# Expert weights in runs of 16 KB, and activations stored in a permuted order

## The chip, the cores and the metric

One core of one Trainium2 chip runs the whole program; the metric is device microseconds of one execution. Before the change three runs took 1560.23, 1564.00 and 1565.98 us, the median being 1564.0 us.

## The reference, cut to what matters

A sequence of 256 tokens (T) of width 1024 (D) passes two blocks, all in float32.

```
# first block
h   = layer_norm(2**0.25 * x + token_mixer(x), ln1)         # attention and a gated MLP
logits = h @ w_router + b_router                            # 32 experts, the best 4 for each token
for each expert e, on the tokens that chose it:
    gt  = min(xb @ w_gate[e] + b_gate[e], 7)                # w_gate, w_up, w_down: 32 x 1024 x 1024
    up  = clip(xb @ w_up[e] + b_up[e], -7, 7)
    hid = gt * sigmoid(1.702 * gt) * (up + 1)
    y   = hid @ w_down[e] + b_down[e]
x   = layer_norm(2**0.25 * h + sum of y * gate, ln2)
# second block: a recurrent mixer and an attention side by side, then a convolved feed-forward of width 2816
```

## The kernel before, in words

**Stages.** `front` computes the first block up to h and the router, `moe` the experts, `tail_norm` the second layer norm, `mixer2` and `ffn2` the second block. The order of the work on each engine is the order in the code. SP issues nearly all loads, in order; a load into a slot waits on SP until the slot's last reader is done.

**Expert weights.** A matrix of 4 MB (1024 rows of 4 KB) comes in four quarters of 1 MB. Quarter i holds rows 256 i to 256 i + 255, and partition p gets rows 256 i + 2p and 256 i + 2p + 1: one run of 8 KB. So the contraction index of chunk k on partition p is row 256 (k // 2) + 2p + k % 2, and the left operands have to be taken in the same order: `pairs(k)` (line 628) is that slice, with a step of two, used by the gather of h (line 710), by the transposes of the hidden values (line 768) and in the overflow loop. There are 384 quarters; `expert_pieces` gives their order: gate and up of expert e, then down of expert e - 1.

**Slots.** 18 slots of 1 MB each, in two pools, hold quarters in turn. In `front` the same slots serve the first block's weights: `pump` (L1260) loads a raw piece and splits it into two float32r parts (`wp`, L1272 on ACT and L1273 on VectorE or POOL); five slots hold small constants and intermediate results (`carve`). As the slots come free, `through` and `freed` load the first 18 quarters of expert weights. In `moe`, `ahead(n)` calls `fetch`, which issues (L188) the refills of all slots whose readers already stand in the code, so that SP runs 18 quarters ahead.

**An expert.** The experts are taken in turn, two to a batch of 128 gathered rows, 64 for each. `gate_up(e)` runs "gate" (tile g) and "up" (tile u), 8 chunks x 2 halves of 512 columns each, and `swiglu` (L757 to L761); `finish(e - 1)` runs "down" (tile y) of the expert before; `hidden_t` transposes the hidden values. After each second expert `gather` (L707 to L713) picks the next batch's rows with one-hots and `scatter` (L728) adds the results into `self.acc`, which is the tile of x. At expert 0 `start_sum` (L916) writes the gated b_down plus 2**0.25 * h there.

**The end of `front`.** For each of the two halves of 128 tokens the layer norm's scale comes from VectorE's steps L97 to L109; `router` takes the logits (L558), their top 8 (L559), scales h on ACT (L560) and adds ln1_b on POOL (L561). The routing's VectorE chain (L665 to L688) and the one-hots (L700) follow, then the first gather.

**The end of `moe`.** After the last "down", loads of ln2_g, ln2_b and norm1_g go into two slots, and `stream` sets up the second block's loads with six of the slots, two for raw pieces and four for parts.

Of the kernel before, what the change touches and what calls it, by code (L numbers as in the profile page):

```python
# [17 lines left out]
OP = mybir.AluOpType  # L18
# [12 lines left out]

SLOTS_A = "r8 c1 c0 c2 c3 c4".split()
SLOTS_B = "r0 r1 r2 r3 r4 r5 r6 r7 h0 h1 h2 h3".split()

REST = 15
RING_A = len(SLOTS_A)
FFN_RAW, FFN_HALF = 4, 4
# [18 lines left out]
def bcast_rows(ap, n, parts=128):  # L56
    return bass.AP(tensor=ap.tensor, offset=ap.offset, ap=[[0, parts], [1, n]])


class Net:  # L60
# [66 lines left out]
    def run(self):  # L127
# [31 lines left out]
        with ExitStack() as fctx:  # L159
            self.front(fctx)  # L160
        self.dump("h", self.h)
# [19 lines left out]

    def piece(self, src, name="w"):

        pool, i = self.rings[self.turn % len(self.rings)]
        self.turn += 1
        t = pool.tile([128, 2048], F32, tag=i, name=self.nm(name))
        for view, ap in src(t):
            self.nc.sync.dma_start(view, ap)  # L188
        return t

    def front(self, fctx):
# [18 lines left out]

        slot = {i: (p, f"s{i}") for p, names in ((self.pa, SLOTS_A), (self.pb, SLOTS_B)) for i in names}
        cs = [slot[f"c{i}"][0].tile([128, 2048], F32, tag=f"sc{i}", name=f"front_c{i}") for i in range(5)]

# [39 lines left out]
        nf = len(spec)  # L253
        work = self.expert_pieces()
        spec += [(2, src) for _, src in work[:len(slot)]]
        L = {}
# [348 lines left out]
        assert len(self.raw) == len(spec) and not self.raw_slots  # L605
        self.rings = [self.held[nf + i] for i in range(len(slot))]
        self.turn = len(slot)
        self.work = work
        self.got = {key: t for (key, _), t in zip(work, self.raw[nf:])}

# [15 lines left out]

    @staticmethod
    def pairs(k):


        i, x = divmod(k, 2)
        return slice(256 * i + x, 256 * i + 256, 2)

    def expert_pieces(self):

        r = []
        for e in range(NE + 1):
            for x, names in ((e, ("w_gate", "w_up")), (e - 1, ("w_down",)), (e, ("w_down",))):
                if x in range(NE) and (len(names) == 2 or (x == e) == (x == REST)):
                    for nme in names:  # L640
                        v = self.a[nme][0, x].rearrange("(i p x) c -> i p x c", p=128, x=2)
                        r += [((x, nme, i), v[i]) for i in range(4)]
        return r

    def fetch(self, n):

        for key, src in self.work[len(self.got):n]:
            t = self.piece(lambda t: [(t.rearrange("p (k c) -> p k c", k=2), src)])
            self.got[key] = t.rearrange("p (k c) -> p k c", k=2)

    def moe(self, mctx):
# [127 lines left out]
        def weights_of(e, nme):  # L779
            return lambda k: self.got[e, nme, k // 2][:, k % 2, :]  # L780

# [67 lines left out]
        def overflow():  # L849
            n = nc.values_load(lists["num"][0:1, 0:1], min_val=0, max_val=NL - 1)  # L850
            with tc.If(n > 0):
                with tc.For_i(0, n, 1) as i:
# [15 lines left out]
                    for k in range(KC):  # L868
                        for t in range(NT):
                            self.mm(p[:, k, :], self.h[:, t, self.pairs(k)], oh[:, t], start=t == 0, stop=t == NT - 1)  # L870
                    nc.vector.tensor_copy(xo, p)

                    def weights(nme):
                        def f(k):
                            w = m2.tile([128, D], F32, tag="wx", bufs=1, name=self.nm("wx"))
                            rows = a[nme][0, bass.ds(e, 1)].rearrange("o (i p x) c -> i x (o p) c", p=128, x=2)
                            nc.gpsimd.dma_start(w, rows[k // 2, k % 2])
                            return w
# [26 lines left out]
        def start_sum():  # L905
# [18 lines left out]
        def ahead(n):  # L924

            self.fetch(done[0] + len(self.rings))
            done[0] += n

        def finish(e):
            b, el = divmod(e, EB)  # L930
            ahead(4)
            if el == 0:
# [43 lines left out]

        def small(*names):
            while self.rings[self.turn % len(self.rings)][0] is self.pa:
                self.turn += 1
            t = self.piece(lambda t: [(t[:, i * D:(i + 1) * D], bcast_rows(a[nme], D)) for i, nme in enumerate(names)])  # L980
            return t[:, 0:D], t[:, D:2 * D]

        self.ln2g, self.ln2b = small("ln2_g", "ln2_b")
        self.n1g, self.junk = small("norm1_g_2")
        flush(sums)
# [216 lines left out]
    def stream(self):  # L1202
# [23 lines left out]
        for f in range(NF + 2):  # L1226
            for q in range(3):
# [3 lines left out]
                if u % 2 == 0:  # L1231
# [5 lines left out]
                               else (lambda t, x=x: t[:, x:x + 1, :])))  # L1237
        self.pieces(spec, halves, [(self.pa, f"s{i}") for i in SLOTS_A[:2]])
        self.half_slots = [(self.pa, f"s{i}") for i in SLOTS_A[2:]]
        self.low = [self.nc.gpsimd]  # L1240
# [8 lines left out]
    def pump(self):  # L1249

        nc = self.nc
        while True:
            while self.raw_slots and len(self.raw) < len(self.spec):
                r = len(self.raw)
                k, src = self.spec[r]
                pool, tag = self.held[r] = self.raw_slots.pop(0)
                n = src.shape[2]
                t = pool.tile([128, 2048], F32, tag=tag, name=self.nm("w"))[:, :k * n]
                t = t.rearrange("p (k c) -> p k c", k=k)
# [8 lines left out]
            k, n = src.shape[1:]  # L1268
            pool, tag = slot = self.half_slots.pop(0)
            t = pool.tile([128, 2, 1024], F32R, tag=tag, name=self.nm("wp"))[:, :, :k * n]  # L1270
            t = t.rearrange("p q (k c) -> p q k c", k=k)
# [650 lines left out]
    def ffn2(self):  # L1922
# [3 lines left out]
        with ExitStack() as c:  # L1926
# [7 lines left out]

            self.raw_slots += [(ph, f"r{i}") for i in range(FFN_RAW)]
            self.pump()
# [6 lines left out]
            self.low = [V]  # L1943
            self.half_slots += [(ph, f"h{i}") for i in range(FFN_HALF)]
            self.pump()
# [60 lines left out]
```

## Time and profile before

| what | value |
|---|---|
| profiled execution | 1563.47 us |
| its span | 1561.9 us |
| mean granted TensorE clock | 0.973 |
| busy: PE, VectorE, ACT, POOL | 1430.0, 598.6, 364.3, 178.4 us |
| HBM read | 488.34 MB |
| loads of w_gate, w_up, w_down | 128 each, 1024 KB, 19.8 us from issue to landing |

PE is TensorE's matmul, PEld its weight load, DVE VectorE, ACT ScalarE, POOL GpSimd, SP the engine that issues loads (SPq: its queue). L77 is the helper through which all matmuls pass, so they are told apart by tiles: g, u and y are the products of the experts. The DMA share is the mean busy share of 16 engines, and it can pass 1. In the timeline a row has its start, its length, engine, line, operation, and the tiles written and read; in brackets stands the idle time before it and what ended that. Groups have busy us, mean ns of one, and the idle time before.

### The profile page before, as it was taken

How to read it: one execution, taken by the hardware profiler on the slowest of the kernel's cores; microseconds unless marked ns; L12 is line 12 of the kernel's file. 1: busy time of each engine (PE TensorE's matmuls, PEld its weight loads, DVE VectorE, ACT ScalarE, POOL GpSimd, SP SyncE). 2: the span in 40 equal slices, each digit the busy share in tenths (PEclk: the TensorE clock that was granted, in tenths of full speed). 3: DMA queues.
4: the chain of work that ended last, by engine and by line, in shares of the span. 5: the costliest groups of instructions: out<-in, count | busy, mean ns of one | idle time of the engine just before them, and what ended most of it. 6: DMA issues, size and time to landing. Idle time of an engine off the chain costs nothing. (4 is left out here: it accounts for less than half of the span.)

```text
span 1561.9 us, 19367 instructions
## 1 busy us (share of the span) xinstructions
PE 1430.0 (92%) x7904; PEld 823.4 (53%) x7904; DVE 598.6 (38%) x1087; ACT 364.3 (23%) x607; POOL 178.4 (11%) x155
## 2 busy tenths in 40 slices
PE   8779999999998889899988989997998999999998
PEld 7664333333333233233333333326877787799998
DVE  5882121122121121112124111116587547876664
ACT  4551010110101000100110100103643323365552
POOL 4630000000000020000000000004353223200000
PEclk9988999999999999999999999998998999999999
DMA  9886999999999999999999999993423125765540
GB/s 300 289 324 270 423 420 421 422 421 421 422 421 421 421 419 416 422 421 421 422 422 420 421 422 422 421 393 104 149 88 118 32 80 173 239 218 180 194 139 28
DMA packets 119280, 491.15 MB, mean 314 GB/s; under 512 B 16391, under 2 KB 46791, under 8 KB 70036
## 3 DMA queue, kind: packets, MB, share of 16 engines
q1 hardware_dynamic: 118304, 489.02, 78.9%
q8 instruction: 63, 1.03, 0.3%
q10 hardware_dynamic: 372, 0.66, 0.1%
q0 software_dynamic: 512, 0.20, 0.1%
q14 instruction: 29, 0.24, 0.0%
HBM read 488.34 MB, written 1.51 MB: 314 GB/s over the span
## 5 line engine op out<-in xcount | busy, mean ns | idle before, releaser
L77 PE MATMUL u<-w,xg 128*64 128x512 f32 x1024 | 231.5, 596 | 17.3 <-DMA w<-in_w_up_dram 17.3
L77 PE MATMUL g<-w,xg 128*64 128x512 f32 x1024 | 238.3, 613 | 9.4 <-DMA w<-in_w_gate_dram 9.4
L77 PE MATMUL y<-w,hidT 128*64 128x512 f32 x1024 | 228.1, 595 | 6.1 <-DMA w<-in_w_down_dram 5.1
L1273 DVE TENSOR_TENSOR wp<-w,wp 128x1024 fp32r<-128x1024 f32 x115 | 151.4, 1342 | 102.0 <-ACT wp L1272 101.8
L1272 ACT CAST wp<-w 128x1024 fp32r<-128x1024 f32 (+1 forms) x148 | 151.6, 1038 | 163.0 <-PE pj L77 59.0
L77 PEld LDWEIGHTS u<-w,xg 128*64 128x64 f32 x1024 | 68.9, 137 | 170.0 <-issue 119.3
L77 PEld LDWEIGHTS g<-w,xg 128*64 128x64 f32 x1024 | 72.3, 141 | 154.8 <-issue 122.3
L77 PEld LDWEIGHTS y<-w,hidT 128*64 128x64 f32 x1024 | 70.3, 137 | 157.7 <-issue 136.9
L1273 POOL TENSOR_TENSOR wp<-w,wp 128x1024 fp32r<-128x1024 f32 (+1 forms) x33 | 79.3, 2410 | 593.0 <-ACT wp L1272 591.0
L777 ACT COPY y<-y 64x512 f32<-64x512 f32 x64 | 37.1, 580 | 375.9 <-PE y L77 375.4
L757 DVE TENSOR_SCALAR g<-g 128x512 f32<-128x512 f32 x32 | 22.1, 691 | 230.3 <-PE g L77 230.3
L770 DVE COPY hidT<-tr 128x256 f32<-128x256 f32 x32 | 13.6, 425 | 236.5 <-ACT hidT L769 236.5
L760 DVE TENSOR_SCALAR g<-u 128x512 f32<-128x512 f32 x32 | 22.1, 692 | 180.5 <-PE u L77 180.5
L77 PE MATMUL pj<-wp,h2p 128*128 128x512 f32 x336 | 84.4, 408 | 1.1 <-DVE wp L1273 0.9
L758 ACT ACTIVATE sg<-g 128x512 f32<-128x512 f32 x32 | 20.2, 630 | 255.1 <-DVE g L757 255.1
L77 PEld LDWEIGHTS pj<-wp,h2p 128*128 128x128 f32 x336 | 64.1, 194 | 17.8 <-DVE wp L1273 1.3
L77 PE MATMUL a<-h3p,wp 128*128 128x256 f32 x528 | 66.9, 283 | 0.5 <-DVE h3p L1308 0.5
L77 PEld LDWEIGHTS a<-h3p,wp 128*128 128x128 f32 x528 | 66.1, 191 | 2.2 <-DVE h3p L1308 0.7
L77 PE MATMUL b<-h3p,wp 128*128 128x256 f32 x528 | 66.9, 283 | 0.0
L77 PEld LDWEIGHTS b<-h3p,wp 128*128 128x128 f32 x528 | 64.9, 192 | 0.0
L77 PE MATMUL sc<-y,ogT 128*128 128x512 f32 x124 | 62.5, 619 | 2.5 <-ACT y L777 1.4
L77 PE MATMUL d<-wp,hid 128*128 128x512 f32 x264 | 63.6, 391 | 0.0
(527 smaller groups left out, 1582.8 us busy)
## 6 DMA issues: line engine op xcount, KB each, us to landing
w<-in_w_gate_dram SPq DMA_DIRECT2D x128, 1024.0 KB, 19.8
w<-in_w_up_dram SPq DMA_DIRECT2D x128, 1024.0 KB, 19.8
w<-in_w_down_dram SPq DMA_DIRECT2D x128, 1024.0 KB, 19.8
w<-in_w_in_dram SPq DMA_DIRECT2D x27, 1024.0 KB, 5.1
w<-in_w_ffn_up_dram SPq DMA_DIRECT2D x22, 1024.0 KB, 5.3
w<-in_w_ffn_down_dram SPq DMA_DIRECT2D x11, 1024.0 KB, 7.7
w<-in_w_out_dram SPq DMA_DIRECT2D x8, 1024.0 KB, 8.7
w<-in_w_branch_b_dram SPq DMA_DIRECT2D x2, 1024.0 KB, 5.0
```

Of the source, the lines that this page charges most:

```text
L77: return self.nc.tensor.matmul(out, lhsT, rhs, start=start, stop=stop)
L757: nc.vector.tensor_scalar(g1, pg, 7.0, None, op0=OP.min)
L758: nc.scalar.activation(sg, g1, AF.Sigmoid, scale=1.702)
L760: nc.vector.tensor_scalar(g1, pu, -7.0, 7.0, op0=OP.max, op1=OP.min)
L770: nc.vector.tensor_copy(hidT[:, 2:4].rearrange("p j f s -> p j (f s)"), p[:, 2:4])
L777: nc.scalar.copy(yv[64 * i:64 * i + 64, hf * 512:(hf + 1) * 512], py[64 * hf:64 * hf + 64, :])
L1272: nc.scalar.copy(t[:, 0], src)
L1273: self.low[j % len(self.low)].tensor_tensor(t[:, 1], src, t[:, 0].bitcast(F32), op=OP.subtract)
```

## The change

A matrix's halves (2 MB) replace quarters as the unit of most loads: partition p gets rows 512 i + 4p to 512 i + 4p + 3, one run of 16 KB. The 18 slots become nine tiles of 16 KB a partition (`PAIRS`); a half of such a tile is a `Slot`. In `front` and in the second block the halves are used singly. In `moe` the first refill of each tile goes into the same tile by quarters, later ones are single loads into a new tile, and the last four quarters again go singly.

The new order of rows (4p + x) would be a slice with a step of four. Instead the columns of h are stored in the order in which the chunks want them: ACT's scale and POOL's addition in `router` write permuted into the tile of x, which becomes `self.h`, and the tile that was h becomes `self.acc`; VectorE's last step in `swiglu` writes permuted into a new tile `hid`; `start_sum` reads h back through the permutation. The gather and the transposes then take plain slices of 128.

```diff
+PAIRS = "r2r3 r4r5 r6r7 r8c1 c0c2 c3c4 r0r1 h2h3 h0h1".split()
+PAIRS_A = PAIRS[3:6]
+EARLY = 2 * len(PAIRS)
-        self.acc = self.x
+        self.acc, self.h = self.h, self.x
+    def double(self, name, dtype=F32):
+        return (self.pa if name in PAIRS_A else self.pb).tile([128, 4096], dtype, tag=name, name=self.nm("w"))
+    def halved(t):
+        return [Slot(t[:, 2048 * x:2048 * x + 2048]) for x in range(2)]
...
         def freed():
             self.freed()
-            if len(self.half) == len(halves):
-                self.raw_slots += self.half_slots
-                self.half_slots = []
-                self.pump()
+            for name in PAIRS[-2:]:
+                pair = [slot[name[:2]], slot[name[2:]]]
+                if len(self.half) == len(halves) and all(i in self.half_slots for i in pair):
...
+                    through(name[:2], name[2:])
...
-            S.activation(r[:, t, :], r[:, t, :], AF.Copy, scale=rs)
-            G.tensor_tensor(r[:, t, :], r[:, t, :], ln1b, op=OP.add)
+            S.activation(self.by_chunks(self.x[:, t, :]), self.by_rows(r[:, t, :]), AF.Copy, scale=rs)
+            G.tensor_tensor(self.by_chunks(self.x[:, t, :]), self.by_chunks(self.x[:, t, :]), self.by_rows(ln1b), op=OP.add)
...
+    def by_chunks(t):
+        return t.rearrange("q (i x p) -> q i p x", x=4, p=128)
+    def by_rows(t):
+        return t.rearrange("q (i p x) -> q i p x", x=4, p=128)
...
     def fetch(self, n):
-        for key, src in self.work[len(self.got):n]:
-            t = self.piece(lambda t: [(t.rearrange("p (k c) -> p k c", k=2), src)])
-            self.got[key] = t.rearrange("p (k c) -> p k c", k=2)
+        while self.turn < n and 2 * self.turn < len(self.work):
+            u = 2 * self.turn
+            name = PAIRS[self.turn % len(PAIRS)]
+            early = u < 2 * EARLY
+            t = (self.early[name] if early else self.double(name)).rearrange("p (k c) -> p k c", k=4)
+            self.turn += 1
+            (key, src), (key1, src1) = self.work[u:u + 2]
+            if not early and u < len(self.work) - 4:
+                e, nme, q = key
+                v = self.a[nme][0, e].rearrange("(i p x) c -> i p x c", p=128, x=4)
+                self.nc.sync.dma_start(t, v[q // 2])
+            else:
+                self.nc.sync.dma_start(t[:, 0:2], src)
+                self.nc.sync.dma_start(t[:, 2:4], src1)
...
-                    self.mm(p[:, c, :], self.h[:, t, self.pairs(c0 + c)],
+                    self.mm(p[:, c, :], self.h[:, t, (c0 + c) * 128:(c0 + c + 1) * 128],
...
-            nc.vector.scalar_tensor_tensor(sg, g1, 1.0, sg, op0=OP.add, op1=OP.mult)
-            return sg
+            hid = m2.tile([128, 512], F32, tag="hid", bufs=1, name=self.nm("hid"))
+            nc.vector.scalar_tensor_tensor(self.by_chunks(hid), self.by_rows(g1), 1.0, self.by_rows(sg),
+                                           op0=OP.add, op1=OP.mult)
+            return hid
...
-                self.tr(p[:, j, :], sg[:, self.pairs(j)])
+                self.tr(p[:, j, :], sg[:, j * 128:(j + 1) * 128])
...
-                    nc.vector.scalar_tensor_tensor(self.acc[:, t, n * 512:(n + 1) * 512],
-                                                   self.h[:, t, n * 512:(n + 1) * 512], ALPHA, p,
-                                                   op0=OP.mult, op1=OP.add)
+                    cs = slice(n * 512, (n + 1) * 512)
+                    nc.vector.scalar_tensor_tensor(self.by_rows(self.acc[:, t, cs]), self.by_chunks(self.h[:, t, cs]),
+                                                   ALPHA, self.by_rows(p), op0=OP.mult, op1=OP.add)
...
-            ahead(8)
+            ahead(2)
```

## Rows read from the trace of the kernel before

**Rows 1.** page: GB/s of 40 equal slices of the span
```profile
GB/s 300 289 324 270 423 420 421 422 421 421 422 421 421 421 419 416 422 421 421 422 422 420 421 422 422 421 393 104 149 88 118 32 80 173 239 218 180 194 139 28
```

**Rows 2.** busy us by engine in a stretch; last: clock, DMA share, GB/s
```profile
300.00:1000.00 700.00, 641.92 (x2990) 236.85 (x2988) 136.99 (x270) 65.85 (x134) 11.01 (x40) 0.99 1.01 421
```

**Rows 3.** waits in 200 to 1000 us: total, times, longest
```profile
PEld u L77 <- DMA w<-in_w_up_dram: 42.5, 33, 1.4
```

**Rows 4.** timeline of two experts: start, us, engine, operation
```profile
403.37 0.38 PE L77 MATMUL u<-bgu,ohb 128*64 128x512 bf16 x2
...
432.37 2.15 PE L77 MATMUL tr<-oh,h 128*128 128x128 f32 x16
...
440.29 7.09 PE L77 MATMUL y<-w,hidT 128*64 128x512 f32 x32
...
457.43 0.38 PE L77 MATMUL u<-bgu,ohb 128*64 128x512 bf16 x2
```

**Rows 5.** DMA of 300 to 500 us: packets, issues, KB, us to landing
```profile
DMA packets 11561, 84.24 MB, mean 421 GB/s; under 512 B 1285, under 2 KB 1285, under 8 KB 1285
...
w<-in_w_gate_dram SPq DMA_DIRECT2D x28, 1024.0 KB, 19.8
```

**Rows 6.** SP's waits at 125:160, one window, landing at 160:180 us
```profile
SPq L188 <- PE g L77: 38.2, 8, 19.2
...
115.00:120.00 5.00, 2.94 (x16) 2.86 (x15) 1.62 (x8) 0.00 (x0) 0.28 (x3) 0.50 0.01 5
...
w<-in_w_gate_dram SPq DMA_DIRECT2D x3, 1024.0 KB, 9.9
```

**Rows 7.** DMA at 10:15, 17.5:22.5 (w_in), 50:55 us (w_out)
```profile
DMA packets 1825, 1.80 MB, mean 360 GB/s; under 512 B 21, under 2 KB 1825, under 8 KB 1825
...
DMA packets 961, 1.93 MB, mean 385 GB/s; under 512 B 27, under 2 KB 27, under 8 KB 960
...
DMA packets 974, 1.94 MB, mean 387 GB/s; under 512 B 29, under 2 KB 29, under 8 KB 974
```

**Rows 8.** timeline of the stage's end
```profile
1029.64 1.94 PE L77 MATMUL u<-w,xg 128*64 128x512 f32 x8 [0.55 <-DMA w<-in_w_up_dram]
1029.66 0.33 SPq L188 DMA_DIRECT2D w<-in_w_down_dram  x1
...
1046.74 7.09 PE L77 MATMUL y<-w,hidT 128*64 128x512 f32 x32
```

**Rows 9.** timeline of the end of the first block
```profile
106.37 1.15 ACT L560 ACTIVATE h<-h,rsi 128x1024 f32<-128x1024 f32 x1
...
106.69 1.42 DVE L543 SCALAR_TENSOR_TENSOR h<-h,lmv,ln1g 128x512 f32<-128x512 f32 x2
...
107.65 2.67 POOL L561 TENSOR_TENSOR h<-h,ln1b 128x1024 f32<-128x1024 f32 x1 [5.87 <-ACT h L560]
...
108.39 1.95 DVE L103 SCALAR_TENSOR_TENSOR rst<-rsi,rsw 128x1 f32<-128x1 f32 x1
...
112.69 2.34 POOL L561 TENSOR_TENSOR h<-h,ln1b 128x1024 f32<-128x1024 f32 x1 [2.37 <-ACT h L560]
112.83 2.23 DVE L676 TENSOR_SCALAR rneed<-rneed 128x2 f32<-128x2 f32 x1
```

**Rows 10.** groups of POOL and VectorE by shape: busy, mean ns, idle before
```profile
L1438 POOL TENSOR_TENSOR tmp<-z 128x1024 f32<-128x1024 f32 x1 | 3.3, 3330 | 3.3 <-DVE z L1433 3.3
...
L700 DVE TENSOR_TENSOR oh<-rk,slot 128x256 f32<-128x256 f32 x16 | 6.7, 416 | 0.7 <-DVEq L851 0.6
...
L916 DVE SCALAR_TENSOR_TENSOR x<-h,sc 128x512 f32<-128x512 f32 x4 | 2.7, 687 | 3.2 <-PE sc L77 3.2
...
L1551 DVE TENSOR_TENSOR TA<-TA 128x225 f32<-128x225 f32 x1 | 0.6, 558 | 0.0
```

**Rows 11.** groups of PE's weight loads
```profile
L77 PEld LDWEIGHTS tr<-oh,h 128*128 128x128 f32 x256 | 32.9, 204 | 15.1 <-issue 15.1
L77 PEld LDWEIGHTS mm<-xp,wp 128*128 128x128 f32 x240 | 31.4, 204 | 4.0 <-ACT wp L1272 2.4 <-DVE wp L1273 1.6
```

More of the change, by code (lines that the diff above doesn't have):

```diff
@@ L57, in bcast_rows, with __init__, room @@
     return bass.AP(tensor=ap.tensor, offset=ap.offset, ap=[[0, parts], [1, n]])
+class Slot:
+    def __init__(self, view=None, pool=None, tag=None, dtype=F32):
+        self.view, self.pool, self.tag, self.dtype = view, pool, tag, dtype
+    def room(self, name):
+        return self.view if self.pool is None else self.pool.tile([128, 2048], self.dtype, tag=self.tag, name=name)
 class Net:
@@ L180, in run @@
         self.ffn2()
[L182 to L189, printed above, removed]
+    def double(self, name, dtype=F32):
+        return (self.pa if name in PAIRS_A else self.pb).tile([128, 4096], dtype, tag=name, name=self.nm("w"))
+    @staticmethod
+    def halved(t):
+        return [Slot(t[:, 2048 * x:2048 * x + 2048]) for x in range(2)]
     def front(self, fctx):
@@ L208, in front @@
         self.warm(bank("o", [128, 128]), warm, WARM[2])
-        slot = {i: (p, f"s{i}") for p, names in ((self.pa, SLOTS_A), (self.pb, SLOTS_B)) for i in names}
-        cs = [slot[f"c{i}"][0].tile([128, 2048], F32, tag=f"sc{i}", name=f"front_c{i}") for i in range(5)]
+        slot, doubles = {}, {}
+        for name in PAIRS:
+            doubles[name] = self.double(name, F32R if name[0] == "h" else F32)
+            slot[name[:2]], slot[name[2:]] = self.halved(doubles[name])
+        cs = [slot[f"c{i}"].view for i in range(5)]
         def carve(i, at, shape):
@@ L253, in front @@
         nf = len(spec)
-        work = self.expert_pieces()
-        spec += [(2, src) for _, src in work[:len(slot)]]
+        work = self.expert_quarters()
+        spec += [(2, src) for _, src in work[:EARLY]]
         L = {}
@@ L332, in freed @@
             self.freed()
-            if len(self.half) == len(halves):
-                self.raw_slots += self.half_slots
-                self.half_slots = []
-                self.pump()
+            for name in PAIRS[-2:]:
+                pair = [slot[name[:2]], slot[name[2:]]]
+                if len(self.half) == len(halves) and all(i in self.half_slots for i in pair):
+                    self.half_slots = [i for i in self.half_slots if i not in pair]
+                    doubles[name] = self.double(name)
+                    slot[name[:2]], slot[name[2:]] = self.halved(doubles[name])
+                    through(name[:2], name[2:])
         def through(*names):
@@ L605, in front @@
         assert len(self.raw) == len(spec) and not self.raw_slots
[L606 to L609, printed above, removed]
+        order = [slot[h] for t in PAIRS for h in (t[:2], t[2:])]
+        assert [self.held[nf + i] for i in range(EARLY)] == order
+        self.work, self.turn, self.got, self.early = work, len(PAIRS), {}, doubles
+        for (key, _), t in zip(work, self.raw[nf:]):
+            self.have(key, t)
     def split_biases(self, bf):
@@ L640, in expert_pieces, with have @@
                     for nme in names:
-                        v = self.a[nme][0, x].rearrange("(i p x) c -> i p x c", p=128, x=2)
-                        r += [((x, nme, i), v[i]) for i in range(4)]
-        return r
+                        v = self.a[nme][0, x].rearrange("(i p x) c -> i p x c", p=128, x=4)
+                        r += [((x, nme, q), v[q // 2][:, 2 * (q % 2):2 * (q % 2) + 2, :]) for q in range(4)]
+        return r
+    def have(self, key, t):
+        for x in range(2):
+            self.got[key[:2] + (2 * key[2] + x,)] = t[:, x, :]
     def fetch(self, n):
-        for key, src in self.work[len(self.got):n]:
-            t = self.piece(lambda t: [(t.rearrange("p (k c) -> p k c", k=2), src)])
-            self.got[key] = t.rearrange("p (k c) -> p k c", k=2)
+        while self.turn < n and 2 * self.turn < len(self.work):
[12 more added lines that the diff above has]
+                self.nc.sync.dma_start(t[:, 2:4], src1)
+            self.have(key, t[:, 0:2])
+            self.have(key1, t[:, 2:4])
     def moe(self, mctx):
@@ L869, in overflow @@
                         for t in range(NT):
-                            self.mm(p[:, k, :], self.h[:, t, self.pairs(k)], oh[:, t], start=t == 0, stop=t == NT - 1)
+                            self.mm(p[:, k, :], self.h[:, t, k * 128:(k + 1) * 128], oh[:, t], start=t == 0, stop=t == NT - 1)
                     nc.vector.tensor_copy(xo, p)
@@ L875, in f @@
                             w = m2.tile([128, D], F32, tag="wx", bufs=1, name=self.nm("wx"))
-                            rows = a[nme][0, bass.ds(e, 1)].rearrange("o (i p x) c -> i x (o p) c", p=128, x=2)
-                            nc.gpsimd.dma_start(w, rows[k // 2, k % 2])
+                            rows = a[nme][0, bass.ds(e, 1)].rearrange("o (i p x) c -> i x (o p) c", p=128, x=4)
+                            nc.gpsimd.dma_start(w, rows[k // 4, k % 4])
                             return w
@@ L924, in ahead @@
         def ahead(n):
-            self.fetch(done[0] + len(self.rings))
-            done[0] += n
+            self.fetch(done[0] + len(PAIRS))
+            done[0] += 2 * n
         def finish(e):
             b, el = divmod(e, EB)
-            ahead(4)
+            ahead(1)
             if el == 0:
@@ L975, in moe @@
         finish(NE - 1)
[L977 to L984, printed above, removed]
+        while PAIRS[self.turn % len(PAIRS)] in PAIRS_A:
+            self.turn += 1
+        t = self.double(PAIRS[self.turn % len(PAIRS)])
+        self.ln2g, self.ln2b, self.n1g, self.junk = (t[:, i * D:(i + 1) * D] for i in range(4))
+        for view, nme in ((self.ln2g, "ln2_g"), (self.ln2b, "ln2_b"), (self.n1g, "norm1_g_2")):
+            nc.sync.dma_start(view, bcast_rows(a[nme], D))
         flush(sums)
@@ L1237, in stream @@
                                else (lambda t, x=x: t[:, x:x + 1, :])))
-        self.pieces(spec, halves, [(self.pa, f"s{i}") for i in SLOTS_A[:2]])
-        self.half_slots = [(self.pa, f"s{i}") for i in SLOTS_A[2:]]
+        raw, *parts = PAIRS_A
+        self.pieces(spec, halves, self.halved(self.double(raw)))
+        self.half_slots = [h for t in parts for h in self.halved(self.double(t, F32R))]
         self.low = [self.nc.gpsimd]
@@ L1255, in pump @@
                 k, src = self.spec[r]
-                pool, tag = self.held[r] = self.raw_slots.pop(0)
+                slot = self.held[r] = self.raw_slots.pop(0)
                 n = src.shape[2]
-                t = pool.tile([128, 2048], F32, tag=tag, name=self.nm("w"))[:, :k * n]
+                t = slot.room(self.nm("w"))[:, :k * n]
                 t = t.rearrange("p (k c) -> p k c", k=k)
@@ L1268, in pump @@
             k, n = src.shape[1:]
-            pool, tag = slot = self.half_slots.pop(0)
-            t = pool.tile([128, 2, 1024], F32R, tag=tag, name=self.nm("wp"))[:, :, :k * n]
+            slot = self.half_slots.pop(0)
+            t = slot.room(self.nm("wp")).rearrange("p (q n) -> p q n", q=2)[:, :, :k * n]
             t = t.rearrange("p q (k c) -> p q k c", k=k)
@@ L1933, in bank @@
                 return ps.tile(shape, F32, tag=tag, bufs=bufs, name=self.nm(tag))
-            self.raw_slots += [(ph, f"r{i}") for i in range(FFN_RAW)]
+            self.raw_slots += [Slot(pool=ph, tag=f"r{i}") for i in range(FFN_RAW)]
             self.pump()
@@ L1943, in ffn2 @@
             self.low = [V]
-            self.half_slots += [(ph, f"h{i}") for i in range(FFN_HALF)]
+            self.half_slots += [Slot(pool=ph, tag=f"h{i}", dtype=F32R) for i in range(FFN_HALF)]
             self.pump()
```

12 lines of the change are left out of this document (3 added, 9 removed).

## The prediction

> **What bounds the kernel now.** I read four views in this order: the page's slices, the windows by stage, the waits inside the long stage, and the timeline of two experts.
>
> The slices [rows 1] show one long stage, about 160 to 1045 us, in which the rate stands at 416 to 423 GB/s; before and after it the rate is lower and uneven. It is the expert weights. The windows [rows 2] give 421 GB/s for 300 to 1000 us at a DMA share of 1.01: the 16 engines are never without a packet. PE counts as 92% busy there, which alone would not tell the two apart. The waits do [rows 3]: what PE waits for and could not shift is the landing of weights. And PE could go faster: on a stretch where it waits for no load, the "up" product of one expert starts at 403.37 us and that of the second expert after it at 457.43 us [rows 4], 54.1 us for two experts; the engines need 2 x 12.58 MB / 421 GB/s = 59.8 us for the same. So the stage is bound by the bytes, with some 10% of room on PE. A gain in the transfer rate passes to the end one for one; a gain on PE there is worth nothing. Packets are whole runs: in 300 to 500 us, 11561 packets less 1285 short ones carry some 84 MB, 8 KB each [rows 5].
>
> Before 160 us the order is the other way round: SP waits for PE to free slots [rows 6], and each us by which the first block ends later delays the stage.
>
> **The change part by part.**
>
> *Runs of 16 KB.* Of 384 quarters (1 MB each) of expert weights, 18 are loaded early, the next 18 and the last 4 stay quarters. The other 344, 360.7 MB, become 172 loads of 2 MB with a run of 16 KB a partition. At 421 GB/s they take 856.8 us now. What does a longer run save? The trace has full queues with two shorter runs: 387 GB/s with 2 KB runs (974 packets, all under 8 KB and all but 29 over 2 KB) and 360 GB/s with 1 KB runs, against 421 GB/s [rows 5, 7]. For one of 16 engines that is 84.7, 45.5 and 311.3 ns a packet. The line through 2 KB and 8 KB has a slope of 36.9 ns per 1000 B (434 GB/s for 16 engines) and 9.1 ns left over per packet; through 1 KB and 8 KB it leaves 7.5 ns. So 16 KB should take 604.3 + 9.1 = 613.5 ns against 2 x 311.3 = 622.6 ns: 427 GB/s, 1.46% less time, 12.5 us (10.4 us by the other line). Bounds: nothing, if what is lost at 8 KB is lost per byte; 25 us, if the rate reaches the slope alone; below nothing, if longer runs collide in HBM (a rival, below). I take 12.5, because the two lines agree.
>
> The Trainium skill ("DMA: Bandwidth & Descriptors", "Why small descriptors are slow") has a fixed cost of about 3 cycles per packet beside 32 B a cycle. By that page 8 KB would lose 3 of 259 cycles and 16 KB 3 of 515, an estimate of 0.6% or 5 us. The rows of this trace have a loss per packet two to three times as large; by that page's the time would be 1562.7 us, between the two of the second rival.
>
> *Waits.* A refill now waits until the whole 2 MB slot is read, not half of it, and behind it on SP stand only later refills, in the end the vectors of the second norm and the next block's weights. In the bound stage that is covered: PE reads a piece as it lands, so of nine double slots some eight are queued or in flight, about 39 us of work, where PE's longest stretch without freeing anything is some 10 us (gather and scatter, 432.4 to 440.3 us, rows 4). Landing takes 19.8 us now [rows 5], which is eight loads of 1 MB at 2.49 us, so ten of the 18 slots are not even used. Thin cover exists only where double refills begin, about 170 us: 4 MB were in flight there (landing 9.9 us, rows 6), and one freed pair comes up to 1.8 us later than its first half. I cost it at nothing; without the cover it is 1.8 us an event, for two or three events.
>
> *The end of the stage.* The last "up" product waits for each quarter: 8 matmuls, 1.94 us, after the last landing at 1029.6 us, and then PE has work without a gap until 1053.8 us [rows 8]. With a double 16 matmuls stand behind the last landing: +1.8 us, on the path. The last "down" stays quarters and had 2 us to spare (its last quarter is needed 5.3 us after 1046.74 us; issued at 1029.66 us it lands about 1049.5 us).
>
> *The permuted write in the router.* ACT's L560 (1.15 us) and POOL's L561 (2.67 and 2.34 us) now write, and POOL reads, with steps of 512 B inside. POOL's length is on the path twice: VectorE's L103 takes 1.95 us in place of 0.2 and ends at 110.34 us with L561 (110.32), and L676 takes 2.23 us and ends at 115.06 with the second L561 (115.03) [rows 9]. Routing, the one-hots, the gather and the first refill stand behind. No row has POOL with such steps. Bounds: 2.34 us, as now, and 3.33 us, the slowest product of that shape on POOL [rows 10]. I take the upper end, since a strided operand is not likely to be free: +1.0 us twice, +2.0 us. ACT I leave at 1.15 us; no row has such a write, and twice the time would add 1.15 us twice (rival 4).
>
> The Trainium skill ("GPSIMD Engine Reference", "Performance pitfalls for Q7 kernels") puts a read with a step over 8 bytes at half as much again. By that page L561 would be 3.5 us and this term an estimate of 2.4 us, with the forecast 0.4 us later; no row here shows it.
>
> *The other strided operands.* VectorE's L916, four times 0.69 us, reads h in steps of 512 B, and L761 writes so. The nearest row with two strided sources in SBUF is L1551: 558 ns for 225 elements, against 416 ns for 256 contiguous ones in L700 [rows 10]; so 0 to 0.35 us each. L916 stands between PE's bias products in a stretch where PE sets the refills: +0.4 us. L761 is followed by a whole "down" product (7 us) before its transposes, so it is hidden. PE's reads with a step of two go away, but they cost nothing: LDWEIGHTS takes 204 ns for h now, and 204 ns for the contiguous activations of the first block [rows 11].
>
> *Slots as halves of a double.* The second block's slots are now views of one tile. Two halves of one tile are tracked apart already: ACT and POOL write h[:, 0] at 106.37 us while VectorE writes h[:, 1] at 106.69 us [rows 9]. Nothing. The last four early quarters now go out when both slots of a pair are free; they went out by twos anyway and landed by 115 us; from there to 120 us the engines move 5 GB/s [rows 6], which covers 5 us.
>
> **Sum.** -12.5 + 1.8 + 2.0 + 0.4 = -8.3 us. The profiled execution took 1563.47 us (span 1561.9, 1.6 us around it), 0.5 us under the median of the runs shown, 1564.0 us. So 1563.5 - 8.3 = 1555.2 us, 0.56% under the median.
>
> **Rivals.**
>
> 1. *The rate rises further* (434 GB/s would be reached when a packet costs nothing beside its bytes). For: the costs are bounds, and half as many loads also halves what is paid per load. Against: the three points lie near one line that keeps its intercept. Between 1542 (25 us gained, 4.2 lost) and 1550.
>
> 2. *The rate hardly moves*: the loss at 8 KB belongs to the bytes, or the run is cut again on its way. For: the points come from short stretches beside other work. Against: 2 KB to 8 KB moved the rate by 9%. Then only the costs are left: 1563.5 + 4.2 = 1567.7; with half the loss per packet, 4.6 ns, 6.3 us come back and it is 1561.4.
>
> 3. *The rate falls*, the slower side. Place: HBM; the 128 runs of a load start 16 KB apart in place of 8 KB, and the engines read several at once. If such streams get in each other's way, all 16 slow down. Price: 8.6 us for each per cent of the 856.8 us. It decides below 419 GB/s: 0.5% lost gives 1572. For: no full queue in the trace reads that far apart at a power of two. Against: 2 KB runs of w_out, whose rows lie 4 KB apart, and of w_in, 7 KB apart, go at 387 and 385 GB/s [rows 7], so a power of two shows no harm there. A loss of 1 to 2% gives 1576 to 1585.
>
> 4. *The strided steps cost more*: POOL twice as long as now (+2.5 us each) and VectorE's blocked with it, and halves of a slot waited for together in the first refills. Then 5 to 8 us more, 1560 to 1564.
>
> **How the numbers follow.** Forecast 0.54 (1551 to 1560), rival 1 0.12, rival 2 0.17, rival 3 0.08, rival 4 0.09. The range to 1567 takes in rival 4, most of rival 2; down to 1546 half of rival 1. About 0.5%, 7.8 us, is what a measurement of this kernel can tell from no change, so faster means under 1556.2: somewhat over half of the forecast and all of rival 1, and a little for runs that spread by 5.8 us: 0.48. Slower, over 1571.8, is rival 3 and the upper edge of 2: 0.11. The rest, 0.41, is same.
>
> **What would show it.** Right: in 300 to 1000 us the rate near 427 GB/s with a share of 1.01 and half as many packets; landing times of a double 30 us and more; PE's share in that stage up by a point; L561 near 3.3 us with L103 and L676 ending with it; the stage's end about 8 us earlier and the second block, some 505 us, unchanged. Wrong: 421 GB/s or less (rivals 2 and 3), slices under full share between 170 and 300 us (the waits), L561 at 2.4 us or 5, or a second block that takes another time than before.

## The result and the profile after

The changed kernel takes 1554.6 us (median of 11 executions, 1548.9 to 1559.3) beside 1562.5 us for the kernel before on the same chip (11, 1560.1 to 1566.4): a ratio of 0.9947 with an interval of 0.9933 to 0.9962, about 8 us less where 8.3 were forecast. Timed once more beside later experiments it had 0.9931 (0.9917 to 0.9945). So it is 0.53% faster, just past the 0.5% that the prediction took as what a measurement can tell.

The profiled execution of after has a span of 1553.1 us. Its windows, as in [rows 2] (busy us of PE, weight loads, VectorE, ACT and POOL, then clock, DMA share and GB/s):

```profile
155.00:160.00 5.00, 5.00 (x26) 1.63 (x24) 1.37 (x2) 0.63 (x1) 0.00 (x0) 1.00 0.95 367
160.00:300.00 140.00, 132.38 (x640) 51.04 (x638) 30.09 (x60) 14.52 (x30) 2.26 (x4) 0.98 1.01 426
300.00:1000.00 700.00, 644.26 (x3042) 238.56 (x3040) 147.72 (x272) 65.79 (x134) 10.98 (x40) 0.99 1.01 427
```

The rate is 427 GB/s where it was 421, and the share is 1.01 from 160 us on: the engines are as full as before and move more. Why they do is in the packets of 300 to 500 us, beside [rows 5]:

```profile
DMA packets 5872, 85.52 MB, mean 428 GB/s; under 512 B 651, under 2 KB 651, under 8 KB 651
...
w<-in_w_gate_dram SPq DMA_DIRECT2D x15, 2048.0 KB, 30.2
```

Half as many packets carry slightly more bytes, and a load of 2 MB (a double, as against a quarter of 1 MB) lands 30.2 us after its issue, so the queue is fuller than before (19.8 us).

The end of the first block, beside [rows 9]: start, length, engine and line. L577 is the old L560, L578 the old L561, L121 and L725 are two steps of VectorE's chain, L689 issues the first refill, the first load of the long stage.

```profile
104.72 2.11 ACT L577 ACTIVATE x<-h,rsi 128x1024 f32<-128x1024 f32 x1
...
106.96 2.87 POOL L578 TENSOR_TENSOR x<-x,ln1b 128x1024 f32<-128x1024 f32 x1 [6.84 <-issue]
107.00 2.84 DVE L121 SCALAR_TENSOR_TENSOR rsi<-rst,rsi 128x1 f32<-128x1 f32 x1
...
110.77 2.05 ACT L577 ACTIVATE x<-h,rsi 128x1024 f32<-128x1024 f32 x1 [2.11 <-DVE rsi L121]
...
112.90 2.87 POOL L578 TENSOR_TENSOR x<-x,ln1b 128x1024 f32<-128x1024 f32 x1 [3.07 <-ACT x L577]
113.10 2.75 DVE L725 TENSOR_TENSOR sel<-rgt,req 128x64 bf16<-128x64 f32 x1
...
115.90 0.24 PE L89 MATMUL u<-sel,bits 128*128 128x32 bf16 x3 [6.78 <-DVE sel L725]
117.08 3.75 PE L89 MATMUL tr<-oh,x 128*128 128x128 f32 x16 [0.94 <-DVE oh L743]
120.63 2.97 PE L89 MATMUL sc<-oh,x 128*128 128x128 f32 x16
```

ACT's scaling has nearly doubled (1.15 before); POOL's step grew by 0.20 and 0.53 us only. VectorE's small steps end with POOL's (109.84 and 109.83; 115.85 and 115.77), as before. But the second one is now L725, the last step of the chain ahead of the routing's matmul; before it was L676, with four more lines of the chain behind it, and the matmul came 1.09 us after POOL's end, now 0.13 us. And the stage's end, beside [rows 8]:

```profile
1017.70 3.65 PE L89 MATMUL u<-w,xg 128*64 128x512 f32 x16 [1.25 <-DMA w<-in_w_up_dram]
...
1036.70 7.09 PE L89 MATMUL y<-w,hidT 128*64 128x512 f32 x32
```

16 matmuls stand behind the last landing instead of 8. The last "down" ends at 1043.79 us, 10.0 us before the old 1053.83. Not all of that is the change: ACT's first scaling, ahead of which no arithmetic was changed, happens to start 1.65 us earlier in this execution (104.72 against 106.37), and the second block happens to take 1.2 us longer (509.3 against 508.1). In the eleven profiles of this document's whole kernels that scaling starts between 104.7 and 109.2 us and the second block takes 506.3 to 509.3 us. Hence I read every experiment over two marks that lie between these: **A**, the start of ACT's first scaling, and **U**, the end of the last "up" product, with the first refill between them:

| kernel | A to first refill | first refill to U | A to U | time, us |
|---|---|---|---|---|
| before | 18.75 | 906.46 | 925.21 | 1562.5 |
| after | 20.98 | 895.65 | 916.63 | 1554.6 |
| after, again | 21.02 | 895.46 | 916.48 | 1552.5 |

The first refills, of before and of after:

```profile
125.12 2.04 SPq L188 DMA_DIRECT2D w<-in_w_down_dram  x2
```

```profile
125.70 0.33 SPq L689 DMA_DIRECT2D w<-in_w_down_dram  x1
```

A to U is 8.6 us shorter, 2.2 us lost at the front and 10.8 us won in the stage. A to U repeats within 0.15 us here and within 0.63 us in the other kernel with two profiles (experiment 3). Where the first refill falls between the marks moves more: by 1.3 us in experiment 4, with the same code there.

### The profile page after: what moved, and what is told of

The parts are those of the page before. It is cut to its first block, busy times and chain, and to the rows that moved or that the text cites. A ratio compares the mean times of both kernels' runs of the same rounds, so it can differ in the third digit from the quotient of the medians.

```text
span 1553.1 us, 19026 instructions
## 1 busy us (share of the span) xinstructions
PE 1421.4 (92%) x7904; PEld 821.1 (53%) x7904; DVE 613.0 (39%) x1087; ACT 365.0 (24%) x607; POOL 179.1 (12%) x155
## 5 line engine op out<-in xcount | busy, mean ns | idle before, releaser
L89 PE MATMUL u<-w,xg 128*64 128x512 f32 x1024 | 227.4, 594 | 17.4 <-DMA w<-in_w_up_dram 17.4
L1316 ACT CAST w<-w 128x1024 fp32r<-128x1024 f32 (+1 forms) x116 | 118.6, 1034 | 147.8 <-PE pj L89 60.9
L1317 POOL TENSOR_TENSOR w<-w,w 128x1024 fp32r<-128x1024 f32 (+1 forms) x33 | 79.5, 2416 | 586.7 <-ACT w L1316 581.5
L1317 DVE TENSOR_TENSOR w<-w,w 128x1024 fp32r<-128x1024 f32 x83 | 112.8, 1377 | 82.6 <-ACT w L1316 82.5
L89 PE MATMUL pj<-w,h2p 128*128 128x512 f32 x336 | 84.3, 408 | 0.9 <-DVE w L1317 0.9
L89 PEld LDWEIGHTS pj<-w,h2p 128*128 128x128 f32 x336 | 64.2, 194 | 17.4 <-DVE w L1317 1.3
L771 DVE TENSOR_TENSOR h<-h,sc 128x512 f32<-128x512 f32 x60 | 41.1, 687 | 28.4 <-PE sc L89 28.4
L1317 DVE TENSOR_TENSOR wp<-w,wp 128x1024 fp32r<-128x1024 f32 x32 | 38.4, 1224 | 18.6 <-ACT wp L1316 18.6
L89 PE MATMUL mm<-w,xp 128*128 128x512 f32 (+1 forms) x168 | 36.8, 379 | 6.3 <-DVE xp L329 6.3
L89 PEld LDWEIGHTS sc<-y,ogT 128*128 128x128 f32 x124 | 20.0, 189 | 37.0 <-DVE h L771 18.6
```

The costliest lines, as they stand in the source:

```text
L89: return self.nc.tensor.matmul(out, lhsT, rhs, start=start, stop=stop)
L771: nc.vector.tensor_tensor(dst, dst, pp[dh], op=OP.add)
L1316: nc.scalar.copy(t[:, 0], src)
L1317: self.low[j % len(self.low)].tensor_tensor(t[:, 1], src, t[:, 0].bitcast(F32), op=OP.subtract)
```

## The experiments

**1. The stream by itself.** Only loads from the expert tensors into one ring, queued full, no arithmetic; one run length after another, as in

```python
    def runs_16k(i):
        v = a["w_up"][0, 10 + i // 2].rearrange("(i p x) c -> i p (x c)", p=128, x=4)
        nc.sync.dma_start(slot(4096), v[i % 2])
```

> Loads alone, no arithmetic, seven stretches with full queues: runs of 2, 4 and 8 KB in loads of 1 MB, 8 KB in loads of 2 MB, 16 KB in loads of 2 MB, 16 KB in loads of 1 MB (64 partitions), 32 KB in loads of 4 MB. Theory (a fixed cost of 9.1 ns per packet beside 36.9 ns per 1000 B): 387, 409, 421, 421, 427, 427 and 431 GB/s, whatever the size of a load. Rival (the cost belongs to the load, so larger loads gain): 8 KB in loads of 2 MB like 16 KB, 427, and 16 KB in loads of 1 MB like 8 KB, 421. Rival (the loss is per byte and the rates of the first block were low because of the work beside them): all seven near 421.

Windows with 2, 4 and 8 KB runs in loads of 1 MB; 8 and 16 KB in loads of 2 MB; 16 KB in loads of 1 MB over 64 partitions; 32 KB in loads of 4 MB:

```profile
5.00:65.00 60.00, 0.00 (x0) 0.00 (x0) 1.00 1.05 387
75.00:150.00 75.00, 0.00 (x0) 0.00 (x0) 1.00 1.03 409
165.00:245.00 80.00, 0.00 (x0) 0.00 (x0) 1.00 1.02 421
270.00:335.00 65.00, 0.00 (x0) 0.00 (x0) 1.00 1.01 422
350.00:425.00 75.00, 0.00 (x0) 0.00 (x0) 1.00 1.01 428
470.00:600.00 130.00, 0.00 (x0) 0.00 (x0) 1.00 1.01 215
680.00:735.00 55.00, 0.00 (x0) 0.00 (x0) 1.00 1.01 434
```

Two comparisons matter. At 8 KB the load's size makes no difference (421 and 422), so the price is one of the packet and not of the load: that part of rival 1 is gone. And from 2 to 16 KB the line of the prediction (9.1 ns a packet and 36.9 ns for each 1000 B) gives 387, 409, 421 and 427 against 387, 409, 421 to 422 and 428. The loads over 64 partitions were expected at the full rate and went at half of it, with the engines busy all the time (1.01): the same packets, each twice as long. So at 16 KB the size of a load is not separated from its run.

**2. Quarters throughout**, all else as in after:

```diff
-            if not early and u < len(self.work) - 4:
+            if False:
```

> The changed kernel with every refill as two loads of 1 MB, runs of 8 KB; slots, permuted activations and all else as changed. Theory (length of the runs): 421 GB/s in 300 to 1000 us, and the time goes back to that of the kernel before plus the costs in the first block, some 1564 us, less nothing at the end since the last up product waits for quarters again. Rival (the double slots or the new order, not the runs): 427 GB/s stays, 1553 to 1555 us.

1565.9 us (10 executions, 1563.4 to 1572.9), ratio 1.002 (1.0008 to 1.0032).

```profile
300.00:1000.00 700.00, 641.35 (x2994) 232.74 (x2992) 145.48 (x270) 65.97 (x134) 11.00 (x40) 0.99 1.01 421
```

The rate is back at 421 and the gain is gone; what is left of the change costs about 3 us. A to U is 928.15 us, 2.9 over before, of which 2.3 lie ahead of the first refill (21.08 us). The edit takes back the size of the loads together with their runs; experiment 1 shows no effect of the size at 8 KB. So the run length brings 11.5 us of A to U.

**3. Only GpSimd writes permuted.** ACT scales in place, contiguous:

```diff
-            S.activation(self.by_chunks(self.x[:, t, :]), self.by_rows(r[:, t, :]), AF.Copy, scale=rs)
-            G.tensor_tensor(self.by_chunks(self.x[:, t, :]), self.by_chunks(self.x[:, t, :]), self.by_rows(ln1b), op=OP.add)
+            S.activation(r[:, t, :], r[:, t, :], AF.Copy, scale=rs)
+            G.tensor_tensor(self.by_chunks(self.x[:, t, :]), self.by_rows(r[:, t, :]), self.by_rows(ln1b), op=OP.add)
```

> ACT scales h in place, with contiguous rows as before the change; POOL alone writes permuted, from contiguous operands. Theory (ACT's strided write took 0.95 us more twice and is what made the start later): L577 near 1.15 us, L578 near 2.9 us, and the span from the start of the first L577 to the first weight load of moe 1 to 2 us shorter than in the changed kernel (21.0 us there, 18.8 us before the change). Rival (POOL's strided operands are the cost): L578 falls to 2.3 to 2.7 us. Rival (the start is not on the path): the span is shorter and the end of the stage does not move.

One execution: 1553.25 us.

```profile
108.11 1.15 ACT L577 ACTIVATE h<-h,rsi 128x1024 f32<-128x1024 f32 x1
109.39 2.70 POOL L578 TENSOR_TENSOR x<-h,ln1b 128x1024 f32<-128x1024 f32 x1 [5.88 <-issue]
113.22 1.15 ACT L577 ACTIVATE h<-h,rsi 128x1024 f32<-128x1024 f32 x1 [1.17 <-DVE rsi L121]
114.45 2.35 POOL L578 TENSOR_TENSOR x<-h,ln1b 128x1024 f32<-128x1024 f32 x1 [2.36 <-ACT h L577]
...
117.89 0.24 PE L89 MATMUL u<-sel,bits 128*128 128x32 bf16 x3 [5.38 <-DVE sel L725]
```

POOL's permuted write alone costs nothing (2.70 and 2.35 against 2.67 and 2.34 before), and ACT is back at 1.15. From A to the routing's first matmul (tile u) it is 9.78 us here, 11.18 in after and 9.75 before: the strided steps cost 1.43 us on this path, and what brings it is ACT's permuted write with the permuted read that POOL then needs. The edit takes both back at once, so the 1.43 us are not split between them. The theory had L577 right; L578 fell to the 2.3 to 2.7 us of the rival. A to U is 914.74 us, 1.9 under after.

**4. The last "up" ends in quarters**: its second double goes as two loads of 1 MB.

```diff
-            if not early and u < len(self.work) - 4:
+            if not early and u < len(self.work) - 4 and u != len(self.work) - 10:
```

> The second double of the last expert's w_up comes as two quarters. Theory (the double puts 16 matmuls behind the last landing): 8 matmuls, 1.9 us, behind it in place of 3.65, and the end of the last product 1.7 us earlier against the last landing. Rival (the quarter lands later by as much): no change against the landing before it.

One execution: 1554.1 us. The product now runs without a gap behind the landing of the first double. A landing is read here from the matmuls that wait for it; below, first of after and then of this run, those behind the first double of w_up for the last expert but one and for the last, and in this run, between them, the issue of the first of the two quarters:

```profile
954.08 3.65 PE L89 MATMUL u<-w,xg 128*64 128x512 f32 x16 [1.02 <-DMA w<-in_w_up_dram]
...
1012.80 3.65 PE L89 MATMUL u<-w,xg 128*64 128x512 f32 x16 [1.02 <-DMA w<-in_w_up_dram]
```

```profile
957.40 3.65 PE L89 MATMUL u<-w,xg 128*64 128x512 f32 x16 [1.02 <-DMA w<-in_w_up_dram]
...
987.52 0.33 SPq L689 DMA_DIRECT2D w<-in_w_up_dram  x1
...
1016.12 7.09 PE L89 MATMUL u<-w,xg 128*64 128x512 f32 x32 [1.02 <-DMA w<-in_w_up_dram]
```

The last matmul ends 7.09 us after the first double's landing, where after has 8.55: 1.46 us sooner, near the 1.7 expected. A to U is 916.40 us all the same, only 0.2 under after, because that landing comes 909.31 us after A, where after has 908.08. The split did not bring this lag. One expert earlier the first double of w_up was already 1.2 us late (850.59 us after A for 849.36), 30 us before the first quarter was issued, and from the landing ahead of it, that of the last w_gate's second double, it follows after 4.89 us in both runs (1007.91 to 1012.80 and 1011.23 to 1016.12). So the edit gives 1.46 us against the stream, and the stream of this execution was late for a reason that stays open.

**5. Both repairs, and the changed kernel beside them**, five rounds each.

> The changed kernel itself, unedited, timed again beside the kernel before and beside the two edits below: about 1554.6 us, ratio to before 0.995. It gives the span between two runs of the same code, against which the two edits are read.

> The changed kernel with both repairs at once: the permuted write is GpSimd's alone, from operands that ScalarE scaled in place contiguously, and the second double of the last w_up goes as quarters. Theory (both steps lie on the path that sets the end): the front gives back 1.9 us (21.0 to 19.1 us from ScalarE's first scaling to the first refill) and the end of the stage 1.5 us, so about 1551.2 us, ratio 0.9925 to 0.993. Rival (the stage's stream sets its own end and takes up what the front gives): 1553 us or more, the u matmuls still 1.5 us closer to their landing, but the stream from first refill to last landing longer by as much.

After 1552.5 us (6 executions, 1550.2 to 1555.3), both repairs 1552.3 us (5, 1552.0 to 1553.0); ratios to before 0.9931 and 0.993. The times tell no difference, so the theory's 1551.2 missed. Over the marks there is one: A to U is 914.70 us, 1.8 under after, but that is experiment 3 alone (914.74 there). The first lines below are of this kernel, the last one of experiment 3:

```profile
123.83 0.33 SPq L689 DMA_DIRECT2D w<-in_w_down_dram  x1
...
953.95 3.65 PE L89 MATMUL u<-w,xg 128*64 128x512 f32 x16 [1.04 <-DMA w<-in_w_up_dram]
...
1012.63 7.09 PE L89 MATMUL u<-w,xg 128*64 128x512 f32 x32 [1.01 <-DMA w<-in_w_up_dram]
```

```profile
955.55 3.65 PE L89 MATMUL u<-w,xg 128*64 128x512 f32 x16 [1.03 <-DMA w<-in_w_up_dram]
```

The first refill comes 18.81 us after A, so the front gives its part. At the end the product runs without a gap, 1.46 us shorter against its first landing; but this landing comes 907.61 us after A (105.02 us), where the two profiles of experiment 3 without this repair have 906.19 and 906.82. Again the lag, 0.8 to 1.4 us, is older than the split: one expert earlier it is 848.93 us for 847.44 and 848.12. So A to U does not show what the second repair is worth, since the stream was late in both executions that have it, ahead of the place where it acts. The rival of this expectation describes the end of the stage (the stream is longer by about what is gained) and not the front; that the repair is the cause is not shown.

**6. First refills as doubles too** (`early = False`).

> The changed kernel with the first refills as doubles too, not as quarters. Theory (cover is thin at the start): a double's issue waits until both of its halves are read, so the first refills leave later and the slices under full DMA share between the first refill and 30 us behind it grow; 1 to 3 us lost there, against some 0.5 us won by 9 more loads of 2 MB at 428 in place of 421 GB/s: 1555 to 1557 us. Rival (the matmuls of the first expert read the halves faster than the queue drains): share 1.0 as early as before, the same time or 0.5 us less, 1554 us.

1553.4 us (4 executions, 1550.2 to 1554.9; ratio 0.993), as after beside it (0.9931). The wait is there: the first refill leaves 22.93 us after A (20.98). But it costs nothing, A to U is 916.29 us:

```profile
125.00:130.00 5.00, 5.00 (x28) 2.10 (x28) 1.59 (x6) 0.37 (x1) 0.00 (x0) 0.99 0.10 30
130.00:160.00 30.00, 28.83 (x122) 9.57 (x120) 9.29 (x12) 3.65 (x6) 0.00 (x0) 0.94 0.92 371
160.00:300.00 140.00, 132.38 (x632) 50.88 (x630) 30.02 (x60) 14.53 (x30) 2.26 (x4) 0.96 1.01 427
```

5 us nearly empty, and then the stage is as full as in after. The rival was right: nothing is won by keeping the first refills as quarters.

**7. Runs of 32 KB** for gate and up, on top of experiment 3: one load of 4 MB for a matrix (two of 2 MB for the last w_up); w_down stays at 16 KB, since its rows come from two column halves that sit in different partitions of hid. Four slots of 4 MB take turns, the ninth double slot is left unused. The core of the edit:

```diff
-                v = self.a[nme][0, e].rearrange("(i p x) c -> i p x c", p=128, x=4)
-                self.nc.sync.dma_start(t, v[q // 2])
+                v = self.a[nme][0, e].rearrange("(p x) c -> p x c", x=8)
+                parts = [(t, v)]
```

> The changed kernel with the gate and up matrices in runs of 32 KB (one load of 4 MB for a matrix, four slots of 4 MB in turn, the ninth double slot unused), w_down as before in 16 KB, activations permuted with a step of eight, and GpSimd's permuted write from the run above. Theory (a price per packet sets the rate): 348 quarters of 1.05 MB, 365 MB, took 852 us at 428 GB/s; two thirds of them at 433 and the rest at 428 take 846 us, so 6 to 7 us less, 431 GB/s between 300 and 1000 us; with 1.9 us from the router about 1546 us. Rival (fewer, coarser slots leave the queue dry): the DMA share falls under 1.0 between 160 and 1000 us, TensorE waits for whole matrices, 1553 us or more.

> The changed kernel with GpSimd alone writing permuted, timed: about 1.9 us under the changed kernel by its path (1551 to 1552.5 us); the base against which the run with 32 KB is read.

1563.2 us (11 executions, 1562.0 to 1565.4; ratio 1.0002, 0.9992 to 1.0012), no faster than before, beside 1554.2 us (5, 1549.5 to 1556.8) for experiment 3 timed. A to U is 924.65 us against 915.37.

```profile
180.00:200.00 20.00, 19.38 (x96) 6.51 (x92) 3.15 (x4) 1.79 (x3) 0.00 (x0) 1.00 0.57 220
...
300.00:1000.00 700.00, 637.61 (x2968) 237.60 (x2966) 144.63 (x268) 65.20 (x133) 11.03 (x40) 0.97 1.00 429
...
181.41 0.33 SPq L729 DMA_DIRECT2D w<-in_w_up_dram  x1
198.80 0.80 SPq L729 DMA_DIRECT2D w<-in_w_down_dram  x2
```

Two things went otherwise. The rate is 429, not 431: the line per packet gives 430.4 GB/s for 32 KB, and with a third of the bytes at 427 just 429; the 434 of experiment 1 came from 55 us of 4 MB loads, whose slices of 10 and 15 us run from 423 to 446, and was too short to lean on. And there is a hole of 8.6 us of stream (20 us at a share of 0.57): the second 4 MB slot is free only when both of its old doubles are, one of them four places later in the turn, and SP stands at that refill from 181 to 199 us. From 160 to 300 us as a whole the rate is 388 GB/s, 426 in experiment 3: an estimate of 12.5 us of stream, of which the higher rate behind it gives some 4 back. That is near the 9.3 us by which A to U is longer.

**8. The same with the slots taken over in another order**, so that each pair of old doubles comes free sooner.

> The run with 32 KB again, but with the four big slots taken over in the order in which their halves come free (r2r3+r4r5, r8c1+c0c2, r6r7+r0r1, h2h3+h0h1 for the first two turns). Theory (the loss was the one hole at the change of slots, 180 to 200 us at a share of 0.57, some 8.6 us of stream): the hole closes to 2 us or less and about 7 us come back, 1554 to 1557 us, the rate between 300 and 1000 us still 429. Rival (four slots of 4 MB are too few all along): the share between 160 and 300 us stays under 0.97 and the time at 1560 us or more.

1559.4 us (10 executions, 1553.5 to 1561.0; ratio 0.9974, 0.9962 to 0.9987): 3.8 us better, half of what was expected.

```profile
160.00:180.00 20.00, 18.04 (x94) 8.30 (x95) 3.20 (x6) 2.65 (x6) 0.00 (x0) 0.91 0.74 310
180.00:200.00 20.00, 18.50 (x94) 6.37 (x92) 4.88 (x12) 2.52 (x5) 0.00 (x0) 1.00 0.98 392
...
300.00:1000.00 700.00, 641.64 (x2986) 238.92 (x2984) 144.95 (x269) 65.79 (x134) 10.98 (x40) 0.97 1.00 429
```

The hole moved to 160 to 180 us, ahead of the first 4 MB load (5 us), and 160 to 300 us as a whole stays at a share of 0.95 and 397 GB/s, so neither side had it whole. A to U is 921.65 us: of the 9.3 us over experiment 3 the order of the slots was 3.0, about a third. That the rest comes from slots of 4 MB being too coarse where they take over from smaller ones fits the low rate there, but no run shows it by itself. In the steady stage 429 against 427 GB/s is worth some 4 us, less than the change of slots took. A version that beats the changed kernel by its time was not found; experiment 3 is 1.1 to 1.9 us shorter from A to U, which its times do not resolve.

## Why the prediction was right

The sum was -8.3 us; the time came down by 8.0 us, A to U by 8.6 us. The large term is right by its mechanism. Of the small ones the end of the stage came as forecast, the router's size by luck, and the other strided operands cost nothing.

- **What bounds the kernel**: right. The rate went up by 1.4% and the stream became 12.5 us shorter (below); PE's busy share rose by a third of a point (644.26 us in the window of [rows 2]), less than the point forecast.
- **Runs of 16 KB, -12.5 us at 427 GB/s**: right in mechanism and size. First refill to U is 10.8 us shorter, and with 1.7 us more behind the last landing (3.65 for 1.94) that is 12.5 us of stream; against experiment 2 it is 13.2 (11.5 and 1.7). Experiment 1 shows the price per packet by itself, and that the size of a load has no part in it at 8 KB; experiment 2 shows that the gain goes when the long runs go. The Trainium skill's 3 cycles per packet ("DMA: Bandwidth & Descriptors", "Why small descriptors are slow") would have given 5 us by the prediction's estimate; the runs show 9.1 ns a packet, as the trace of before did.
- **Waits, nothing**: right; the share is 1.01 from 160 us on, and even doubles in the first refills (experiment 6) cost nothing, though SP waits there, earlier still than where the prediction saw the cover as thin.
- **End of the stage, +1.8 us**: 1.7 (3.65 us behind the last landing for 1.94). Against the landings 1.46 us of it come back when the last double is split (experiment 4); no run shows that in A to U or in the time.
- **Router, +2.0 us**: the size was nearly right (2.2 us), the place was wrong, and that the two fit is luck. The prediction put the cost on POOL (3.3 us for 2.67 and 2.34) and left ACT at 1.15; by its own rows that upper bound is 0.66 and 0.99 us, 1.65 in all, not 1.0 twice. In fact POOL takes 2.87 us with strided reads and writes, 2.70 and 2.35 with the write alone, and ACT 2.1 us, the case that stood in rival 4. The two ACT steps are longer by 0.96 and 0.90 us and POOL's by 0.20 and 0.53; of these 2.6 us 1.43 reach the routing's first matmul, since VectorE's chain gets further before POOL's second step holds it. The other 0.8 us lies in the first gather, where PE begins at the 1.2 GHz level (granted 0.50 from 115 to 120 us in both kernels) after a wait of 6.78 us (5.35 before). From 120 to 125 us the granted clock is 0.72, before it was 0.89, and the last 16 matmuls of the gather took 2.97 us for 2.18. They take 2.97 to 3.20 us in four of the five profiles with the strided steps and 2.10 to 2.53 in the six without; but in experiment 4, with the strided steps, they took 1.95, with the clock at 0.79 from 120 to 125 us. So this part goes with the change in most executions and is not shown to be the change's. Nor is it shown to reach the end: in experiment 4 the first refill came 19.65 us after A, yet the third expert's "up" began 78.3 us after A, in after 78.1. The Trainium skill's rule ("GPSIMD Engine Reference", "Performance pitfalls for Q7 kernels"), half as much again for a strided read, is not what POOL shows here: 7% and 23%.

The two windows (columns as above) and the 16 matmuls, of before; the window of after, whose matmuls stand in its first timeline; the matmuls of experiment 4:

```profile
120.00:125.00 5.00, 5.00 (x33) 3.65 (x34) 2.01 (x7) 0.74 (x2) 0.00 (x0) 0.89 0.09 29
...
120.85 2.18 PE L77 MATMUL sc<-oh,h 128*128 128x128 f32 x16
```

```profile
120.00:125.00 5.00, 5.00 (x28) 4.00 (x29) 1.59 (x6) 0.74 (x2) 0.00 (x0) 0.72 0.02 3
```

```profile
122.42 1.95 PE L89 MATMUL sc<-oh,x 128*128 128x128 f32 x16
```

- **Other strided operands, +0.4 us**: L962 (L916 before) takes 1.0 us for 0.69, but from the first bias product to expert 0's next product it is 6.19 us where it was 6.40. So nothing, PE sets that stretch. L805 (L761 before) takes 1064 ns for 692, hidden as said.

```profile
139.56 1.98 PE L89 MATMUL sc<-bdn,gT 32*128 32x512 f32 x4 [0.45 <-ACT gT L956]
140.72 1.96 DVE L962 SCALAR_TENSOR_TENSOR h<-x,sc 128x512 f32<-128x512 f32 x2 [1.02 <-PE sc L89]
...
145.75 1.06 PE L89 MATMUL g<-w,xg 128*64 128x512 f32 x2
...
L805 DVE SCALAR_TENSOR_TENSOR hid<-g,sg 128x512 f32<-128x512 f32 x32 | 34.0, 1064 | 1.1
```

- **Second block unchanged**: 509.3 us, 507.4 in the second profile of the same code, 508.1 before: no more than the spread.

The rivals: the first, second and third fell with the rate of 427 in the kernel; of the first, experiment 1 adds that nothing is saved per load at 8 KB. The fourth held in ACT's step alone, POOL's did not double.

## What to carry to other kernels

Where the engines are full, compare rates at two run lengths in the same trace: if they lie on one line per packet, that line tells what a longer run brings, here to within a tenth of the gain. Ask of a longer run what it does to the slots; the second doubling was worth 2 GB/s and cost more than that when coarse slots were taken over. Read small costs between marks inside the profile: the time of an execution spreads by 5 us and more, the stretch between the marks came out 0.15 and 0.63 us apart where the same code was profiled twice. And before a late landing is put down to an edit, look whether the landings ahead of the edit were late already.

## What was not expected of the hardware

- Loads of 1 MB over 64 of the 128 partitions with runs of 16 KB went at 215 GB/s, with all engines busy, against 428 over 128 partitions.
- ACT takes 2.05 to 2.11 us for 128x1024 written in steps of 512 B, 1.15 us contiguous. VectorE takes 1.0 us in place of 0.69 for 128x512 with such steps; POOL's permuted write from contiguous operands cost nothing, with the operand read permuted too it took 2.87 us.
